# Five groups of projection columns in place of six in a two-layer hybrid decoder, with some tiles reassigned

## The chip, the cores and the metric

The kernel runs on one core of one Trainium2 chip. The metric is device time in microseconds (us) of one execution, lower being better. Inputs and weights, all in single precision, lie in HBM at the start, and the result is written back to HBM.

## The reference

Two layers are applied to a sequence of 256 tokens with 1024 features. In each layer one input projection feeds three groups of heads: mLSTM, MoBA block attention and NSA sparse attention.

```python
for l in range(DEPTH):                                # DEPTH = 2
    h = rmsnorm(x, norm_mix[l])                       # x: 256 x 1024
    proj = h @ w_in[l]                                # w_in: 1024 x 3476
    (m_q, m_k, m_v, m_o, m_i, m_f, b_q, b_k, b_v,     # 4 x 512, 4, 4, 3 x 256
     n_q, n_kc, n_vc, n_ks, n_vs, n_kw, n_vw, n_g) = split(proj)   # 256, 6 x 64, 12
    y_m = mlstm(silu(conv(m_q, m_k)), m_v, m_o, m_i, m_f)
    y_b = moba(b_q, b_k, b_v)
    y_n = nsa(n_q, n_kc, n_vc, n_ks, n_vs, n_kw, n_vw, n_g, cmp_pe[l], ...)
    x = x + concat(y_m, y_b, y_n) @ w_out[l]
    h = rmsnorm(x, norm_ffn[l])
    x = x + square(relu(h @ w_ff1[l])) @ w_ff2[l]     # 1024 -> 4096 -> 1024
```

NSA compresses `n_kc` and `n_vc` with a small network whose inputs get learned positions (`cmp_pe`) added.

## The kernel before, in words

**Matmuls.** Operands are single precision, split into a high part (`hi`, rounded to the format that TensorE takes in one pass) and a low part (`lo`, the rest). A product is three matmuls: high by high, high by low, low by high (`passes`). Tokens are two tiles of 128 (`i` is 0 or 1) and the features are eight tiles of 128 (`k`), so a group of columns that is projected with tokens on the partitions takes 2 x 8 x 3 = 48 matmuls per layer, each with as many moving columns as the group has (`project`).

**Groups.** The 3476 columns of `w_in` are taken in groups (`GROUPS`, line 378): o1 holds NSA's queries and the inputs of its compression (384 columns), o2 the rest of NSA (268: selected and window keys and values, gates), o3 the mLSTM gates and MoBA's queries (264), o4 MoBA's keys and values (512), o5 mLSTM's values (512), o6 its output gate (512). mLSTM's queries and keys are q0 to q3, 256 columns each, projected the other way round (`project_t`: 48 matmuls of 256 columns). c0 to c3 are pieces of the compression network; c0 and c1 run as one burst, and so do c2 and c3. `ORDER` (line 30) is the order on TensorE: o1, o6, o2, o3, c0, c1, q0, c2, c3, o4, q1, q2, q3, o5.

**Weights.** The loads are cut into pieces: four per o group (two feature tiles each), two per q group (four each). A piece is loaded by SP into one of five `raw` tiles (RAW_BUFS, line 32), cast to `hi` by ScalarE (the very first piece by VectorE, in two chunks), and VectorE makes `lo`. There are six tiles of each part. A `raw` tile comes free when the `lo` is made, a part when its last matmul is done. So the load of a piece waits for the `lo` of the piece five earlier. The compression weights go to two `whole` tiles and are not split. One queue, SP's, issues all the weight loads in order.

**PSUM and other tiles.** Results of the o and q groups go to two `acc` banks, other results to six `wk` banks. The two banks of an o group are freed by the process that reads them: `cmp_inputs` (line 899) for o1, `nsa_heads` (line 934) for o2, `gates` (line 1003) for o3, `moba_heads` for o4. `cmp_inputs` copies NSA's queries to two `R` tiles, which `nsa_heads` frees after its normalisation; the pool has only these two. `gates` then takes two `R` tiles for MoBA's queries, so that its copies wait for NSA's normalisation. The `Y` tiles (two) hold mLSTM's output before its transposition (`numerators`). The positions are loaded in `first_smalls` (line 793) to a `dg` tile, after four small loads.

**Order of instructions.** `Flow` is a list planner that runs when the program is written: each process yields operations with planned costs, the planner keeps a planned clock for every engine and issues the operation that can begin first, with preference by rank. Each engine then executes its instructions in that fixed order. `due` (lines 392 to 428) gives each piece a due time, and the casts are placed by it (AHEAD, line 32). The planner's cost of a power on GpSimd, which makes the reciprocal root of `rsqrt`, is 0.3 us and 0.165 us for each value in a row.

**NSA's chain.** For each token tile: copies from PSUM (`R`, `VS`, `GT`), squares (`th`), sums (`hss`), the power (`hr`, on GpSimd), scaling (`N`), rotation, transposes on TensorE to `QK`, and then the scores, a burst of matmuls on `QK`.

Of the kernel before, what the change touches and what calls it, by code (L numbers as in the profile page):

```python
# [26 lines left out]
K_ID, K_TRI, K_NM, K_NMT, K_NMC, K_COS, K_SIN, K_VAL, K_CS, K_END = 0, 128, 256, 384, 512, 544, 576, 608, 612, 868  # L27


ORDER = ("o1", "o6", "o2", "o3", "c0", "c1", "q0", "c2", "c3", "o4", "q1", "q2", "q3", "o5")  # L30

RAW_BUFS, PART_BUFS, AHEAD = 5, 6, 1.3

# [111 lines left out]
class Flow:  # L145
# [25 lines left out]
    def free(self, *tiles):  # L171
        for t in tiles:
            name = t.tensor.name
            self.places[self.owner.pop(name)].append(self.used.get(name, ("", 0.0))[1])
# [108 lines left out]
def body(ctx, tc, x, w_in, b_if, conv_qk, m_norm, moba_g, nsa_qg, nsa_kg, cmp_pe, cmp_w1, cmp_w2,  # L283
# [18 lines left out]
    def new(tag, *shape, dt=F32):  # L302
        return New(tag, (128, *shape), dt)
# [6 lines left out]
    def keep(tag, *shape, dt=F32, parts=128):  # L310

        if tag not in kept:
            kept[tag] = cp.tile([parts, *shape], dt, tag=tag, name=tag)
        return kept[tag]
# [60 lines left out]
    def rows(w, k0, kk, c0, n):  # L375
        return [(w[k0 * 128:(k0 + kk) * 128, c0:c0 + n].rearrange("(k p) n -> p k n", p=128), None)], kk, n

    GROUPS = {"o1": (C_NQ, 384), "o2": (C_KS, 268), "o3": (C_G, 264), "o4": (C_BK, 512), "o5": (C_MV, 512),
              "o6": (C_MO, 512)}
    WO_ORDER = [6, 7, 4, 5, 0, 1, 2, 3]  # L380
    NCH = DFF // 256

# [11 lines left out]
    for l in range(DEPTH):  # L394
        for name in ORDER:
            if name[0] == "c":
                s = int(name[1])
                pieces.append(([(cmp_w1[l, a, s * 512:(s + 1) * 512, :].rearrange("(k p) n -> p k n", p=128), a)
                                for a in range(2)], 8, 128))
                due.append(t)  # L400
                t += 0.45
            elif name[0] == "q":
                pieces += [rows(w_in[l], 4 * s, 4, int(name[1]) * 256, 256) for s in range(2)]
                due += [t, t + 12 * 288 / 2400]
                t += 48 * 288 / 2400
            else:
                n = GROUPS[name][1]
                pieces += [rows(w_in[l], 2 * s, 2, *GROUPS[name]) for s in range(4)]
                due += [t + 6 * s * (n + 32) / 2400 for s in range(4)]
                t += 48 * (n + 32) / 2400  # L410
        pieces += [rows(w_out[l], k, 1, 0, D) for k in WO_ORDER]
        due += [t + 6 * k * 544 / 2400 for k in range(4)] + [t + (48 + 3 * k) * 544 / 2400 for k in range(4)]
        t += 96 * 544 / 2400
        for kind, c, a in FF_ORDER:
            if kind == "up":
                pieces.append(rows(w_ff1[l], 4 * a, 4, c * 256, 256))
                due.append(t)
                t += (8 * 544 + 8 * 288) / 2400
            else:
                if a == 0:  # L420
                    pieces += [rows(w_ff2[l], 2 * c + f, 1, 0, D) for f in range(2)]
                    due += [t, t + 3 * 544 / 2400]
                t += 12 * 544 / 2400

    whole = {j for j, p in enumerate(pieces) if len(p[0]) == 2}
    raws, parts = {}, {}
    coming = [0, 0]
    taken = [0]
# [1 line left out]
    def loads(unsplit):  # L430

        for j, (srcs, kk, n) in enumerate(pieces):
            if (j in whole) != unsplit:
                continue
            if j < 4:
                yield f"before {j}"
            elif unsplit:
                yield f"raw {j - 1}"
            raw = yield new("whole" if j in whole else "raw", 1024)
            raws[j] = raw  # L440
            for src, a in srcs:
                dst = raw[:, :kk * n] if a is None else raw[:, a * 512:(a + 1) * 512]
                yield sy.dma_start(dst.rearrange("p (k n) -> p k n", n=n), src)
            done.add(f"raw {j}")

    def chunks(j):
# [74 lines left out]
    class Layer:  # L521
        def __init__(self):
            self.o, self.held, self.W, self.Y = {}, {}, {}, {}
            self.rs = [keep(f"rs{i}", 1) for i in range(2)]
            self.r2 = [keep(f"r2{i}", 1) for i in range(2)]
            for name, shape, dt in (("H", (8, 2, S), F32R), ("Mh", (8, S), F32R),
                                    ("Ml", (8, S), F32R), ("QK", (10, S), F32), ("RB", (S,), F32),
                                    ("VS", (2, 2, 64), F32), ("VB", (2, 256), F32), ("VM", (2, 4, 130), F32),
                                    ("VC", (4, 64), F32), ("KCT", (2, 16), F32), ("em", (2, 4), F32),
                                    ("cg", (2, 64), F32), ("mr", (384,), F32R)):  # L530
                setattr(self, name, keep(name, *shape, dt=dt))
            self.GT = [keep(f"GT{i}", 12) for i in range(2)]

            self.Hh, self.Hl = (self.H[:, :, a, :] for a in range(2))
            self.Fh, self.Fl = self.Hh, self.Hl

    Ls = [Layer() for _ in range(DEPTH)]

# [253 lines left out]

    def first_smalls():
        yield "H017"
        yield from small_loads(0, 0)
        yield gp.tensor_copy(B[:, 0:128], ident)
        yield gp.tensor_copy(B[:, 128:416], C[:, K_NM - 128:K_NM + 160])
        per = yield new("dg", 128)
        yield sy.dma_start(per[:64], cmp_pe.rearrange("l a (i j) d -> (l a i) (j d)", j=2))
        pps = yield wk()  # L800
        yield tr(pps[:, :64], per[:64], ident[:64, :64])
        yield dv.tensor_copy(PEs, pps[:, :64].rearrange("p (l a i) -> p l a i", l=2, a=2))
        free(pps, per)
        done.add("s00")
        yield "o100"
        yield from small_loads(0, 1)
        done.add("s10")
        for l in range(1, DEPTH):
            yield f"F{l - 1}17"
            for part in range(2):  # L810
                yield from small_loads(l, part)
                done.add(f"s{part}{l}")
# [86 lines left out]
    def cmp_inputs(l):  # L899
        L = Ls[l]  # L900
        L.R = []
        KV = []
        for i in range(2):
            yield f"o1{l}{i}"
            yield f"rs{l}{i}"
            o = L.o["o1"][i]
            KV.append((yield new("KV", 2, 2, 64)))
            yield act(KV[i], o[:, 256:384].rearrange("p (a d) -> p a d", a=2)[:, :, None, :].to_broadcast([128, 2, 2, 64]),
                      AF.Copy, scale=L.rs[i])
            L.R.append((yield new("R", 8, 64)))  # L910
            yield act(L.R[i][:, 0:4].rearrange("p a d -> p (a d)"), o[:, 0:256], AF.Copy, scale=L.rs[i])
            free(o)
            done.add(f"R{l}{i}")
        yield f"s0{l}"

        Xt = yield new("MQ", 2048)
        yield gp.memset(Xt[:, :1024], 0.0)
        X = Xt[:, :1024].rearrange("p (i a c) -> p i a c", i=16, a=2)
        for a in range(2):
            kt = yield wk(S)  # L920
            for i in range(2):
                yield tr(kt[:, tokens(i)], KV[i][:, a].rearrange("p b d -> p (b d)"), ident)
            for j in range(2):
                src = kt[64 * j:64 * j + 64, :]
                src = bass.AP(tensor=src.tensor, offset=src.offset + j, ap=[src.ap[0], [2, 16], [16, NCMP]])
                yield tt(X[64 * j:64 * j + 64, :, a, :NCMP], src,
                         PEs[64 * j:64 * j + 64, l, a, :][:, :, None].to_broadcast([64, 16, NCMP]), op=ALU.add)
            free(kt)
        free(*KV)
        L.Xt, L.X = Xt, X  # L930
        done.add(f"X{l}")


    def nsa_heads(l, i):
# [2 lines left out]
        yield f"o2{l}{i}"  # L937
        yield f"s0{l}"
        o, R, GT = L.o["o2"][i], L.R[i], L.GT[i]
        kv = o[:, 0:256].rearrange("p (a b d) -> p a b d", a=2, b=2)  # L940
        yield act(R[:, 4:6], kv[:, :, 0, :], AF.Copy, scale=L.rs[i])
        yield act(L.VS[:, i], kv[:, :, 1, :], AF.Copy, scale=L.rs[i])

        yield ts(GT, o[:, 256:268], L.rs[i], 0.5, op0=ALU.mult, op1=ALU.mult)
        free(o)
        N = yield new("N", 10, 64)
        yield from normed(N, R[:, 0:6], 6, i, ((0, 4, 2, 1), (4, 2, 4, 2)))
        free(R)
# [54 lines left out]
    def gates(l):  # L1003
# [3 lines left out]
        yield f"s1{l}"  # L1007
        L.R2 = []
        for i in range(2):
            yield f"o3{l}{i}"  # L1010
            yield f"rs{l}{i}"
            o = L.o["o3"][i]
            yield stt(GI[:, i], o[:, 0:8], L.rs[i], BIFs[:, l], op0=ALU.mult, op1=ALU.add)
            L.R2.append((yield new("R", 8, 64)))
            yield act(L.R2[i][:, 0:4].rearrange("p a d -> p (a d)"), o[:, 8:264], AF.Copy, scale=L.rs[i])
            free(o)
            done.add(f"bq{l}{i}")
        fg = GI[:, :, 4:8]
        lf, fa, cg, em, BC = keep("lf", 2, 4), keep("fa", 2, 4), L.cg, L.em, keep("BC", 2, 4)
# [422 lines left out]
```

## Time and profile before

| what | value |
|---|---|
| median of 3 executions | 639.02 us (638.28 to 639.03) |
| the profiled execution | 639.09 us |
| its span, first to last instruction | 637.3 us |
| mean granted TensorE clock | 0.999 of full speed |
| TensorE busy | 629.8 us, 99% of the span, 3799 matmuls |
| VectorE, ScalarE, GpSimd busy | 443.3, 366.6, 30.0 us |
| moved by DMA | 112.78 MB, mean 177 GB/s |

The span lies within the profiled execution's time, with 1.8 us around it. A matmul's record is longer than the distance to the next one, because matmuls are pipelined: the distance between starts, and not the record's length, is what a matmul costs TensorE.

### The profile page before, as it was taken

The numbers are of one execution on the slowest core, as the hardware profiler recorded it, in microseconds if no ns is written. First come the engines' busy times: TensorE is split into PE (matmuls) and PEld (weight loads), VectorE is DVE, ScalarE is ACT, GpSimd is POOL, SyncE is SP. The second block draws the span as 40 slices with busy tenths as digits, with TensorE's granted clock in tenths as the row PEclk, the third lists the DMA queues.
The fourth block names the chain that finished last, engine by engine and source line by source line (L and its number), as shares of the span: only waits on it lengthen the run. The fifth ranks groups of instructions, "written<-read, shape, count | busy, mean of one in ns | idle before, by whom it ended". The sixth has DMA issues, their size and how long they took to land.

```text
span 637.3 us, 10219 instructions
## 1 busy us (share of the span) xinstructions
PE 629.8 (99%) x3799; PEld 544.1 (85%) x3799; DVE 443.3 (70%) x823; ACT 366.6 (58%) x718; POOL 30.0 (5%) x50
## 2 busy tenths in 40 slices
PE   9999999999999999999999999999999999999997
PEld 8898898888888888888899879988888888888885
DVE  6778899678574656656594879987776565665661
ACT  7679685655464535444465886845645554545440
POOL 1010200100000000000010111001000000000000
PEclk9999999999999999999999999999999999999999
DMA  8896524349565565646456924254466556564601
GB/s 310 238 304 210 156 67 140 124 137 284 170 203 194 182 211 160 216 163 200 125 153 212 301 69 142 69 167 152 154 212 212 184 187 209 167 214 156 222 34 67
DMA packets 79378, 112.78 MB, mean 177 GB/s; under 512 B 4928, under 2 KB 61792, under 8 KB 79328
## 3 DMA queue, kind: packets, MB, share of 16 engines
q1 hardware_dynamic: 79152, 112.05, 55.5%
q8 instruction: 30, 0.49, 0.3%
q14 instruction: 20, 0.16, 0.1%
q10 hardware_dynamic: 176, 0.07, 0.0%
HBM read 111.06 MB, written 1.05 MB: 176 GB/s over the span
## 4 chain that ended last, share of the span: by engine, by line
PE 91%; DMA 3%; ACT 2%; DVE 2%; issue 1%; POOL 1%; SPq 0%; ACTq 0%; DVEq 0%; POOLq 0%
PE wk L137 57%; PE acc L137 35%; DMA raw<-in_w_in 2%; ACT hi L137 1%; DVE lo L137 1%; DMA ident<-in_cst 1%; POOL hr L137 0%; SPq L136 0%; DVE N L137 0%; ACT QK L137 0%; POOL rs L137 0%; DVE dg L137 0%; ACT R L137 0%; DVE x L137 0%; DVE hss L137 0%
## 5 line engine op out<-in xcount | busy, mean ns | idle before, releaser
L137 DVE TENSOR_TENSOR lo<-raw,hi 128x1024 fp32r<-128x1024 f32 (+4 forms) x209 | 240.4, 1167 | 123.3 <-ACT hi L137 122.6
L137 ACT CAST hi<-raw 128x1024 fp32r<-128x1024 f32 (+3 forms) x207 | 205.9, 1015 | 135.0 <-PE wk L137 111.7
L137 PE MATMUL wk<-H,hi 128*128 128x512 f32 x512 | 128.0, 391 | 0.0
L137 PEld LDWEIGHTS wk<-H,hi 128*128 128x128 f32 x512 | 93.7, 188 | 17.9
L137 PE MATMUL acc<-hi,H 128*128 128x512 f32 (+3 forms) x368 | 99.2, 351 | 0.0
L137 PE MATMUL acc<-hi,P 128*128 128x512 f32 x240 | 79.3, 391 | 0.2 <-DVE P L137 0.2
L137 PE MATMUL wk<-hi,P 128*128 128x512 f32 x240 | 78.8, 389 | 0.0
L137 PEld LDWEIGHTS wk<-H,lo 128*128 128x128 f32 x512 | 69.9, 190 | 5.0
L137 PE MATMUL wk<-H,lo 128*128 128x256 f32 x512 | 71.4, 282 | 0.0
L137 PEld LDWEIGHTS acc<-hi,H 128*128 128x128 f32 x368 | 64.0, 188 | 6.5 <-issue 0.4
L137 PE MATMUL acc<-lo,H 128*128 128x512 f32 (+3 forms) x184 | 65.3, 355 | 0.0
L137 PEld LDWEIGHTS acc<-hi,P 128*128 128x128 f32 x240 | 45.1, 188 | 9.4 <-DVE P L137 0.6
L137 PEld LDWEIGHTS wk<-hi,P 128*128 128x128 f32 x240 | 45.0, 188 | 9.4
L137 PE MATMUL acc<-H,hi 128*128 128x256 f32 x256 | 51.5, 292 | 0.0
L137 PE MATMUL acc<-lo,P 128*128 128x512 f32 x120 | 47.0, 392 | 0.0
L137 PE MATMUL wk<-lo,P 128*128 128x512 f32 x120 | 46.7, 389 | 0.0
L137 ACT COPY th<-wk 128x256 f32<-128x256 f32 x64 | 23.9, 373 | 35.7 <-PE wk L137 35.7
L137 PEld LDWEIGHTS acc<-H,hi 128*128 128x128 f32 x256 | 40.7, 190 | 0.5 <-ACT hi L137 0.2
L137 PEld LDWEIGHTS acc<-lo,H 128*128 128x128 f32 x184 | 34.6, 188 | 3.4 <-issue 0.3
L137 PE MATMUL acc<-H,lo 128*128 128x256 f32 x128 | 36.7, 287 | 0.0
L137 ACT ACTIVATE H<-wk,V 128x128 fp32r<-128x128 f32 x64 | 18.1, 375 | 21.1 <-PE wk L137 21.1
L137 ACT CAST P<-cv 128x512 fp32r<-128x512 f32 x30 | 18.6, 621 | 17.3 <-DVE cv L137 17.3
(199 smaller groups left out, 799.5 us busy)
## 6 DMA issues: line engine op xcount, KB each, us to landing
raw<-in_w_ff SPq DMA_DIRECT2D x128, 512.0 KB, 4.4
raw<-in_w_in SPq DMA_DIRECT2D x40, 512.0 KB, 5.0
raw<-in_w_out SPq DMA_DIRECT2D x16, 512.0 KB, 4.0
whole<-in_cmp_w SPq DMA_DIRECT2D x16, 256.0 KB, 5.0
raw<-in_w_in SPq DMA_DIRECT2D x8, 384.0 KB, 3.9
raw<-in_w_in SPq DMA_DIRECT2D x8, 268.0 KB, 3.5
raw<-in_w_in SPq DMA_DIRECT2D x8, 264.0 KB, 3.2
out<-x SPq DMA_DIRECT2D x4, 256.0 KB, 2.0
```

The costliest lines, as they stand in the source:

```text
L137: o = Op(self.name, lambda: f(out, *args, **kw), outs, ins, self.cost(op, outs, ins))
```

## The change

The 64 columns of NSA's selected keys go from o2 to o1, and o3 is merged into o2. The groups are now o1 of 448 columns, o2 of 468 (window keys and both values, NSA's gates, then mLSTM's gates and MoBA's queries), and o4, o5 and o6 as before. A piece of o2 comes in two loads, one for each of two runs of columns (204 and 264). A bank of o2 is freed when both `nsa_heads` and `gates` have read it. MoBA's queries go to `Y` tiles, and the positions to a `Y` tile too, with the load issued ahead of the four small ones.

```diff
-ORDER = ("o1", "o6", "o2", "o3", "c0", "c1", "q0", "c2", "c3", "o4", "q1", "q2", "q3", "o5")
+ORDER = ("o1", "o6", "o2", "c0", "c1", "q0", "c2", "c3", "o4", "q1", "q2", "q3", "o5")
...
-    GROUPS = {"o1": (C_NQ, 384), "o2": (C_KS, 268), "o3": (C_G, 264), "o4": (C_BK, 512), "o5": (C_MV, 512),
-              "o6": (C_MO, 512)}
+
+    GROUPS = {"o1": (C_NQ, 448), "o2": (C_KS + 64, 468), "o4": (C_BK, 512), "o5": (C_MV, 512), "o6": (C_MO, 512)}
...
-                pieces += [rows(w_in[l], 2 * s, 2, *GROUPS[name]) for s in range(4)]
+                if name == "o2":
+                    pieces += [([(w_in[l, 256 * s:256 * s + 256, c0:c0 + m].rearrange("(k p) n -> p k n", p=128),
+                                      slice(at, at + m)) for c0, m, at in ((C_KS + 64, 204, 0), (C_G, 264, 204))], 2, n)
+                                   for s in range(4)]
+                else:
+                    pieces += [rows(w_in[l], 2 * s, 2, *GROUPS[name]) for s in range(4)]
...
+            self.left = [2, 2]
...
+        def read(self, i):
+
+            self.left[i] -= 1
+            if not self.left[i]:
+                free(self.o["o2"][i])
...
     def first_smalls():
         yield "H017"
+        per = yield new("Y", 512)
+        yield sy.dma_start(per[:64, :128], cmp_pe.rearrange("l a (i j) d -> (l a i) (j d)", j=2))
         yield from small_loads(0, 0)
         yield gp.tensor_copy(B[:, 0:128], ident)
         yield gp.tensor_copy(B[:, 128:416], C[:, K_NM - 128:K_NM + 160])
-        per = yield new("dg", 128)
-        yield sy.dma_start(per[:64], cmp_pe.rearrange("l a (i j) d -> (l a i) (j d)", j=2))
...
             yield act(L.R[i][:, 0:4].rearrange("p a d -> p (a d)"), o[:, 0:256], AF.Copy, scale=L.rs[i])
+            yield act(L.R[i][:, 4], o[:, 384:448], AF.Copy, scale=L.rs[i])
...
-        kv = o[:, 0:256].rearrange("p (a b d) -> p a b d", a=2, b=2)
-        yield act(R[:, 4:6], kv[:, :, 0, :], AF.Copy, scale=L.rs[i])
-        yield act(L.VS[:, i], kv[:, :, 1, :], AF.Copy, scale=L.rs[i])
-
-        yield ts(GT, o[:, 256:268], L.rs[i], 0.5, op0=ALU.mult, op1=ALU.mult)
-        free(o)
+        yield act(R[:, 5], o[:, 64:128], AF.Copy, scale=L.rs[i])
+        yield act(L.VS[:, i], o[:, 0:256].rearrange("p (a b) -> p a b", a=2)[:, :, 0:64], AF.Copy, scale=L.rs[i])
+
+        yield ts(GT, o[:, 192:204], L.rs[i], 0.5, op0=ALU.mult, op1=ALU.mult)
+        L.read(i)
...
-            yield f"o3{l}{i}"
+            yield f"o2{l}{i}"
             yield f"rs{l}{i}"
-            o = L.o["o3"][i]
-            yield stt(GI[:, i], o[:, 0:8], L.rs[i], BIFs[:, l], op0=ALU.mult, op1=ALU.add)
-            L.R2.append((yield new("R", 8, 64)))
-            yield act(L.R2[i][:, 0:4].rearrange("p a d -> p (a d)"), o[:, 8:264], AF.Copy, scale=L.rs[i])
-            free(o)
+            o = L.o["o2"][i]
+            yield stt(GI[:, i], o[:, 204:212], L.rs[i], BIFs[:, l], op0=ALU.mult, op1=ALU.add)
+            L.R2.append((yield new("Y", 8, 64)))
+            yield act(L.R2[i][:, 0:4].rearrange("p a d -> p (a d)"), o[:, 212:468], AF.Copy, scale=L.rs[i])
+            L.read(i)
```

The rest of the diff lets the loading loop write a run of columns of a piece, and recognises a compression piece by its eight tiles.

## Rows read from the trace of the kernel before

**Rows 1.** The page, parts 1 and 4: busy time and the chain of waits by engine.

```profile
PE 629.8 (99%) x3799; PEld 544.1 (85%) x3799; DVE 443.3 (70%) x823; ACT 366.6 (58%) x718; POOL 30.0 (5%) x50
...
PE 91%; DMA 3%; ACT 2%; DVE 2%; issue 1%; POOL 1%; SPq 0%; ACTq 0%; DVEq 0%; POOLq 0%
```

**Rows 2.** Windows: us, busy time of each engine, clock, DMA share, GB/s.

```profile
28.90:40.60 11.70, 11.70 (x98) 11.64 (x96) 6.06 (x19) 7.05 (x14) 2.15 (x2) 1.00 1.01 327
...
330.50:341.70 11.20, 11.20 (x52) 9.15 (x52) 4.75 (x10) 3.99 (x7) 0.00 (x0) 1.00 0.42 119
341.70:353.50 11.80, 11.80 (x98) 11.62 (x97) 7.71 (x21) 8.07 (x16) 1.62 (x2) 1.00 1.02 349
```

**Rows 3.** Timeline of TensorE, second layer: start us, length us, operation, count.

```profile
323.41 0.33 PE L137 MATMUL acc<-lo,H 128*128 128x384 f32 x1
...
327.05 0.33 PE L137 MATMUL acc<-lo,H 128*128 128x384 f32 x1
...
335.84 0.39 PE L137 MATMUL acc<-lo,H 128*128 128x512 f32 x1
...
341.28 0.39 PE L137 MATMUL acc<-lo,H 128*128 128x512 f32 x1
...
341.86 0.28 PE L137 MATMUL acc<-lo,H 128*128 128x268 f32 x1
...
347.31 0.29 PE L137 MATMUL acc<-lo,H 128*128 128x268 f32 x1
...
347.67 0.28 PE L137 MATMUL acc<-lo,H 128*128 128x264 f32 x1
...
353.17 0.28 PE L137 MATMUL acc<-lo,H 128*128 128x264 f32 x1
```

**Rows 4.** The start: timeline of VectorE, PE and SP, and tiles raw and lo.

```profile
5.35 0.62 DVE L137 CAST hi<-raw 128x384 fp32r<-128x384 f32 x2
...
7.21 0.30 PEld L137 LDWEIGHTS acc<-hi,H 128*128 128x128 f32 x2 [0.18 <-DVE H L137]
...
9.70 0.23 PE L137 MATMUL wk<-B 128*128 128x128 bf16 x1
...
18.56 0.50 SPq L136 DMA_DIRECT2D dg<-in_cmp_pe  x1
...
L137 DVE TENSOR_TENSOR lo<-raw,hi x4: 551/750/959, 5.9 to 11.0; 128x384 fp32r<-128x384 f32 x2, 128x768 fp32r<-128x768 f32 x2
...
DMA to landing us min/median/max: 3.9/3.9/3.9
```

**Rows 5.** The chain of waits in order of time: start us, us, what.

```profile
30.79 8.27 DMA raw<-in_w_in
...
342.12 5.68 DMA raw<-in_w_in
...
353.22 2.63 POOL hr L137
```

**Rows 6.** Timeline of TensorE around three stalls, idle time and releaser in brackets.

```profile
44.21 0.38 PE L137 MATMUL acc<-H,lo 128*128 128x256 f32 x1
44.80 1.16 PE L137 MATMUL wk<-QK 64*128 64x128 f32 x16 [0.21 <-ACT QK L137]
...
356.35 0.28 PE L137 MATMUL acc<-H,lo 128*128 128x256 f32 x1
357.29 0.44 PE L137 MATMUL wk<-ident,N 128*128 128x128 f32 x2 [0.66 <-DVE N L137]
...
358.63 0.28 PE L137 MATMUL acc<-H,hi 128*128 128x256 f32 x1
359.25 1.16 PE L137 MATMUL wk<-QK 64*128 64x128 f32 x16 [0.34 <-ACT QK L137]
```

**Rows 7.** ScalarE's copy of MoBA's queries, second layer, and GpSimd's powers of tile hr.

```profile
353.10 0.47 ACT L137 ACTIVATE R<-acc,rs 128x256 f32<-128x256 f32 x1 [0.37 <-DVE GI L137]
...
L137 POOL TENSOR_TENSOR hr<-hss,negh x8: 1333/1635/2617, 35.8 to 387.0; 128x6 f32<-128x6 f32 x4, 128x8 f32<-128x8 f32 x4
```

More of the change, by code (lines that the diff above doesn't have):

```diff
@@ L423, in body @@
                 t += 12 * 544 / 2400
-    whole = {j for j, p in enumerate(pieces) if len(p[0]) == 2}
+    whole = {j for j, p in enumerate(pieces) if p[1] == 8}
     raws, parts = {}, {}
@@ L441, in loads @@
             for src, a in srcs:
-                dst = raw[:, :kk * n] if a is None else raw[:, a * 512:(a + 1) * 512]
-                yield sy.dma_start(dst.rearrange("p (k n) -> p k n", n=n), src)
+                dst = raw[:, a * 512:(a + 1) * 512] if j in whole else raw[:, :kk * n]
+                dst = dst.rearrange("p (k n) -> p k n", n=n)
+                yield sy.dma_start(dst[:, :, a] if isinstance(a, slice) else dst, src)
             done.add(f"raw {j}")
@@ L797, in first_smalls @@
         yield gp.tensor_copy(B[:, 128:416], C[:, K_NM - 128:K_NM + 160])
-        per = yield new("dg", 128)
-        yield sy.dma_start(per[:64], cmp_pe.rearrange("l a (i j) d -> (l a i) (j d)", j=2))
         pps = yield wk()
-        yield tr(pps[:, :64], per[:64], ident[:64, :64])
+        yield tr(pps[:, :64], per[:64, :128], ident[:64, :64])
         yield dv.tensor_copy(PEs, pps[:, :64].rearrange("p (l a i) -> p l a i", l=2, a=2))
```

## The prediction

> **What bounds the kernel now.** I read the page first. TensorE is busy 99% of the span, and the chain of waits that ends last runs on it for 91% [rows 1]. So a change is worth what it takes from TensorE's own stream of matmuls, plus what it takes from or adds to the few places where that stream stands still. The windows come second, for the stages around the change: the granted clock is 1.00, which is the 2.4 GHz level, and TensorE is busy for the whole of the stretches of o2 and o3 [rows 2]. There the DMA engines are busy too: a share of 1.01 and 1.02, with 327 and 349 GB/s, while the stretch of o6 just before has 0.42 and 119 GB/s in the second layer [rows 2]. Third is TensorE's timeline in the second layer, which gives the distance from one matmul to the next by number of columns [rows 3]. Last are the chain of waits and the timeline around the places where TensorE stood still after o3 [rows 5, 6].
>
> **What a matmul costs.** Rows that show the same operation some periods apart give the distance. 384 columns: 327.05 - 323.41 = 3.64 us for 21 matmuls, 173.3 ns. 512 columns: 341.28 - 335.84 = 5.44 us for 24, 226.7 ns. 268: 347.31 - 341.86 = 5.45 us for 45, 121.1 ns. 264: 353.17 - 347.67 = 5.50 us for 45, 122.2 ns [rows 3]. From 384 to 512 columns the slope is 53.4 / 128 = 0.417 ns a column, one column per cycle at 2.4 GHz, and 13.3 ns of each matmul do not depend on its columns. At 268 and 264 columns the same subtraction leaves 121.1 - 111.7 = 9.4 and 122.2 - 110.0 = 12.2 ns.
>
> **Fewer matmuls.** Three groups of 48 matmuls become two, with the same 916 columns in all. Before, a layer spends 48 x (173.3 + 121.1 + 122.2) = 20.00 us on them. After, with the fixed part of the nearest wide rows, 448 columns cost 186.7 + 13.3 = 200.0 ns and 468 cost 195.0 + 13.3 = 208.3, so 48 x 408.3 = 19.60 us: 0.40 us less. With 9.4 ns as the fixed part, which the rows allow as the low end, it is 48 x 400.5 = 19.22 us: 0.78 us less. 448 is a multiple of 64 as 384 and 512 are, and I give it their part; 468 is not, as 268 isn't, and I give it 9.4: 19.41 us. I take 0.5 us a layer, **1.0 us in two layers**, with ends of 0.8 and 1.6. All of it lies on the path, since TensorE never rests there [rows 2].
>
> A rule of the Trainium skill would make more of this. TensorE: Matmul & The Clock Gate, section Back-to-back issue gap, gives sustained spacings of about 81 ns at 128 columns and 131 ns at 512, which is 64 ns of fixed part, and by it the 96 matmuls saved would be worth an estimated 6.2 us. The same section's formula for an isolated matmul has a fixed 2.5 ns, by which they would be worth an estimated 0.2 us. The rows above, with 226.7 ns at 512 columns, agree with neither, and the sum goes by the rows.
>
> **The first piece.** At the start VectorE casts the first piece in two chunks of 384 columns, 0.62 us for both, and then takes the low parts in two more at 0.551 us each [rows 4]. Low parts of 384 and 768 columns take 551 and 959 ns [rows 4], so 1.06 ns a column, and 64 more columns cost 0.07 us in each of four instructions: 0.27 us. TensorE waits for VectorE just behind them, 0.18 us at 7.21 [rows 4], so this is on the path. Its load has 448 KB in place of 384; it landed 3.9 us after its issue [rows 4], and 64 KB more are 0.2 us at the 327 GB/s of a full stretch [rows 2], so the high end is 0.5. The low end is nothing: at 9.70 a filler matmul runs because the next operands are not there [rows 4], and a later start with more work per piece may only fill that hole. I take **0.2 us more**.
>
> **The loads of q0.** The chain of waits goes through a weight load for 8.27 us in the first layer and 5.68 in the second [rows 5]; both end just ahead of q0's first casts. The reason is in the order of pieces: five raw tiles mean that q0's first load waits for the low part of the piece five earlier, which is o2's last. In the new order the piece five earlier is o6's last, a whole group sooner, and o2's pieces of 468 KB put more bytes into the stretch of o6, where the DMA engines had room [rows 2]. So q0's casts should no longer wait for data, and what stands behind them on ScalarE and VectorE comes earlier.
>
> **The copies of MoBA's queries.** In the second layer ScalarE's copy runs only at 353.10 [rows 7], though o3's first half is done before 351, because the R tile has to come free. In Y tiles it waits for nothing but PSUM and its engine. The bank freed by it is q0's, and the new order leaves the second half of o2 and a burst between, some 6 us, so q0 has no new wait.
>
> **The stalls.** TensorE stands still three times just after the merged groups. From the last regular matmul plus its 120 ns to the next: 44.33 to 44.80 is 0.47 us, 356.47 to 357.29 is 0.82, 358.75 to 359.25 is 0.50, together 1.79 [rows 6]. Two wait for ScalarE's copy of transposed queries, one for NSA's scaled heads. If the loads alone set them, all 1.79 us go; if others of the same kind take their place nothing goes; if NSA's later start doubles them, 1.79 us are added. Behind the longest stands GpSimd's power, 2.63 us in the chain [rows 5] against 1.333 for the shortest [rows 7]; that remains. The first-layer stall is the one nearest to the loads, with only a copy behind casts. I take **0.7 us less**: it goes, and the others shrink by a sixth.
>
> **At no cost.** Four casts and four low parts fewer per layer, each a little wider; two more small copies per layer, each under the 0.47 us of a 256-column one [rows 7]; ScalarE and VectorE are each busy about 8 of 11.8 us there [rows 2]. Without that slack a copy would delay a cast by its length. Loads stay at eight per layer for these groups. On SP the positions' load moves ahead of four small loads and of the weight loads between; its issue takes 0.50 us [rows 4], so those are issued half a microsecond later, covered by o1's and o6's matmuls. The dg tile it no longer holds only helps the row scales.
>
> **Sum.** -1.0 + 0.2 - 0.7 = -1.5 us. The profiled execution took 639.09 us, a span of 637.3 and 1.8 around it, and is 0.07 above the median of 639.02. 639.09 - 1.5 = 637.6.
>
> **The rivals.** *The stalls stay.* The planner fixes the order beforehand, and with other times other matmuls stand early in the queue. Then 639.09 - 1.0 + 0.2 = 638.3, with 637.5 to 638.8 by the bounds of the two terms. For it: the power on GpSimd is still there. Against: the loads of q0 are released a group earlier.
>
> *Slower, by NSA's chain.* The second half of o2 now ends later: in the second layer o1 takes 48 x 26.7 ns = 1.3 us more and o2 10.0 us in place of 5.8, so it ends near 353 and not 347.5, with o3 no longer behind it as cover. Copies, squares, sums, power and scaling of that tile then run beside q0, where scores and transposes of the first tile also go. If the planner again counts the power as about 1.3 us and it takes 2.6 [rows 7], each matmul queued behind is early by 1.3 us. To be slower by more than 0.2% (1.28 us, about what a measurement of this kernel can tell from no change) it takes 1.28 + 0.8 = 2.1 us of new standing still, three stalls of the size of the largest. That would be about 640.5. Against: q0, o4 and q1 are there as filling work, and the first layer had only one such stall.
>
> *All three stalls go*: 639.09 - 1.0 + 0.2 - 1.8 = 636.5. For it: both chains pass through the loads [rows 5].
>
> *The change doesn't do what it says*: wide matmuls cost no more than the 173.3 ns of 384 columns [rows 3]. A layer would save 48 x (416.6 - 346.6) = 3.4 us, giving 639.09 - 6.7 = 632.4. Against: 512 columns take 226.7. The Trainium skill's sustained spacings, in the section named, would point this way.
>
> **How the numbers follow.** The forecast, stalls shrunk, has 0.45 (637.0 to 638.2, mostly below 637.74, the bound of 0.2%); stalls stay 0.34, nearly all within 0.2%; all stalls go 0.11; slower 0.09; cheap wide matmuls 0.01. Faster: 0.36 + 0.02 + 0.11 + 0.01 = 0.50. Within: 0.09 + 0.32 = 0.41. Slower: 0.09. The range runs from 636.3, all stalls gone with the higher saving, to 639.5, stalls kept at the upper bounds and one more of 0.7 us added; it leaves out the slower case and the cheap matmuls. The likeliest case's own range is 637.0 to 638.2.
>
> **What would show it.** In the changed profile: 96 matmuls fewer in these groups, 448 and 468 columns at about 200 and 204 to 208 ns; the first projection matmul about 0.2 us later; q0's casts without a wait for a load; no stall before the first layer's scores; MoBA's queries copied soon after their bank is done. Wrong would be a spacing of 468 columns above 210 ns, new stalls of over 0.8 us before transposes or scores in either layer, or out projections that wait for NSA.

## The result, and the profile after

The kernel after takes 646.67 us (median of 4 runs, 645.87 to 646.98) where the kernel before takes 638.65 in the same comparison: a ratio of 1.0118, with a 95% interval from 1.0104 to 1.0132. It is 8 us slower, and the prediction had 637.6 with a range up to 639.5. The profiled execution took 645.87 us, a span of 644.1.

The page of the kernel after, parts 1, 2 (TensorE's granted clock) and 4, answers to [rows 1]:

```profile
PE 633.2 (98%) x3700; PEld 542.7 (84%) x3700; DVE 444.5 (69%) x815; ACT 368.0 (57%) x714; POOL 31.2 (5%) x50
...
PEclk9988999999999999999999999999999999999999
...
PE 87%; DVE 3%; DMA 3%; ACT 3%; issue 2%; POOL 1%; SPq 0%; ACTq 0%; DVEq 0%; POOLq 0%
```

There are fewer matmuls (3700 in place of 3799, some records missing in both), yet TensorE is busy for 3.4 us longer, and its share of the chain falls from 91% to 87%. The two 8s in the clock say where to look: the slices from 32 to 64 us. The second layer takes no part in the loss. From its first projection matmul to the end of the span it takes 644.09 - 328.47 = 315.62 us, against 637.31 - 320.25 = 317.06 before. All is lost in the first layer, and the windows of the kernel after show it (us, busy time of each engine, clock, DMA share, GB/s; they answer to [rows 2], and the last two are o6 and o2 of the second layer):

```profile
31.00:33.30 2.30, 2.30 (x12) 2.05 (x11) 0.00 (x0) 0.00 (x0) 0.00 (x0) 1.00 0.74 183
33.30:36.90 3.60, 1.42 (x6) 0.67 (x5) 1.25 (x2) 2.46 (x3) 0.00 (x0) 1.00 0.96 268
36.90:40.50 3.60, 3.60 (x11) 3.09 (x10) 1.09 (x2) 0.69 (x1) 0.00 (x0) 0.53 1.05 330
40.60:45.00 4.40, 4.40 (x22) 3.89 (x21) 2.59 (x3) 2.42 (x4) 0.00 (x0) 1.00 1.07 377
50.00:58.00 8.00, 5.98 (x46) 5.54 (x48) 6.54 (x23) 6.87 (x16) 1.81 (x4) 0.79 1.03 315
339.98:351.37 11.39, 11.39 (x54) 9.32 (x52) 6.30 (x11) 4.57 (x7) 0.00 (x0) 1.00 0.71 204
351.37:361.69 10.32, 10.32 (x49) 8.83 (x48) 5.92 (x9) 7.09 (x10) 1.33 (x1) 1.00 0.91 316
```

The merged group of 468 columns takes 10.32 us in the second layer and 14.58 in the first, from 30.98 to 45.56. First TensorE stands still, then it runs at half clock. Its timeline in the first layer (start us, length us, and in brackets the idle time and what ended it):

```profile
33.32 0.38 PE L137 MATMUL acc<-hi,H 128*128 128x468 f32 x1
35.19 0.48 PE L137 MATMUL acc<-hi,H 128*128 128x468 f32 x1 [1.49 <-ACT hi L137]
36.35 0.48 PE L137 MATMUL acc<-lo,H 128*128 128x468 f32 x1 [0.69 <-DVE lo L137]
...
37.25 0.59 PE L137 MATMUL acc<-lo,H 128*128 128x468 f32 x1
...
38.42 0.59 PE L137 MATMUL acc<-lo,H 128*128 128x468 f32 x1
...
52.65 0.44 PE L137 MATMUL wk<-ident,KV 128*128 128x128 f32 x2 [1.85 <-ACT KV L137]
```

The two stops are 1.49 + 0.69 = 2.18 us. After them three matmuls take 38.42 - 37.25 = 1.17 us, 390 ns each, where 213 is the second layer's value; eleven of those are another 1.9 us. A further stop of 1.85 us follows at 52.65, and again a stretch of low clock, 0.79 from 50 to 58.

What ended the first stop is the cast of a weight piece on ScalarE, and what ended the second is the low part of the same piece, made behind that cast. The cast was late because another cast stands ahead of it in ScalarE's order, that of another input (`in_sel`), which waited 4.54 us for its own load. The cast of the next piece then waited 0.65 us for the piece's load:

```profile
33.64 0.62 ACT L137 CAST SEL<-th 128x512 fp32r<-128x512 f32 x1 [4.54 <-DMA th<-in_sel]
34.17 0.97 ACT L137 CAST hi<-raw 128x936 fp32r<-128x936 f32 x1
35.78 0.97 ACT L137 CAST hi<-raw 128x936 fp32r<-128x936 f32 x1 [0.65 <-DMA raw<-in_w_in]
```

The chain of waits in order of time, and SP's timeline, show why these loads were late:

```profile
21.64 3.04 DMA raw<-in_w_in
24.70 0.37 SPq L136
...
25.16 2.83 DMA raw<-in_w_in
28.01 0.37 SPq L136
...
28.47 3.01 DMA raw<-in_w_in
31.50 0.38 SPq L136
...
34.17 6.91 DMA raw<-in_w_in
```

```profile
16.96 11.93 SPq L136 DMA_DIRECT2D raw<-in_w_in  x7
...
29.92 0.43 SPq L136 DMA_DIRECT2D th<-in_sel  x1
...
34.17 2.45 SPq L136 DMA_DIRECT2D raw<-in_w_in  x2
```

The pattern is load, issue, load, issue: SP lets the first load of a pair land before it issues the second. Seven issues take 11.93 us. Each piece of o2 now comes in two loads, 204 and 264 columns wide, into one tile, and the list of waits in the built program has the second of each pair wait for the first:

```
24 L136 DMA raw<-in_w_in 128x2x204 [waits DMAHW1_49,DVE_49]
25 L136 DMA raw<-in_w_in 128x2x264 [waits DMAHW2_49,DMAHW1_49]
```

The `DMAHW` semaphores tell of landings, and it is load 24 whose landing load 25 waits for on `DMAHW1_49`. The two loads write different columns, but with rows of 468 columns the built program has the second wait for the first. In the built program, row lengths of 448, 456, 464, 472 and 480 have no such wait; 460, 466 to 470 and 476 have it. (The program uses eight of these semaphores in turn, so a load also waits for the one eight places ahead of it. That is the other landing in both lists, and the kernel before has such waits too.) Everything behind the pairs on SP is late too. That includes `in_sel`, issued at 29.92, and q0's two loads, issued at 34.17. The chain of waits goes on from q0's load to the stop of 1.85 us:

```profile
41.16 1.06 ACT hi L137
...
49.37 0.47 DVE N L137
...
52.19 0.41 ACT KV L137
```

By the Trainium skill, DMA: Bandwidth & Descriptors, section Anatomy of one DMA — SWDGE (gpsimd) path, the DMA engines themselves do not wait on semaphores; a wait is spent on the issuing sequencer. That section describes loads issued by GpSimd, but the chain's rows on SP agree: the time between two issues is SP's, 2.83 to 3.04 us for each pair.

### The profile page after: what moved, and what is told of

It is laid out like the page before. It is cut to its first block, busy times and chain, and to the rows that moved or that the text cites. A ratio compares the mean times of both kernels' runs of the same rounds, so it can differ in the third digit from the quotient of the medians.

```text
span 644.1 us, 10002 instructions
## 1 busy us (share of the span) xinstructions
PE 633.2 (98%) x3700; PEld 542.7 (84%) x3700; DVE 444.5 (69%) x815; ACT 368.0 (57%) x714; POOL 31.2 (5%) x50
## 4 chain that ended last, share of the span: by engine, by line
PE 87%; DVE 3%; DMA 3%; ACT 3%; issue 2%; POOL 1%; SPq 0%; ACTq 0%; DVEq 0%; POOLq 0%
PE wk L137 54%; PE acc L137 33%; DMA raw<-in_w_in 2%; DVE lo L137 1%; POOL hr L137 1%; DVE N L137 1%; ACT hi L137 1%; ACT P L137 1%; DMA ident<-in_cst 1%; SPq L136 0%; DVE H L137 0%; POOL rs L137 0%; ACT H L137 0%; DVE t L137 0%; ACT Y L137 0%
## 5 line engine op out<-in xcount | busy, mean ns | idle before, releaser
L137 DVE TENSOR_TENSOR lo<-raw,hi 128x1024 fp32r<-128x1024 f32 (+3 forms) x201 | 239.2, 1208 | 132.6 <-ACT hi L137 131.6
L137 ACT CAST hi<-raw 128x1024 fp32r<-128x1024 f32 (+2 forms) x199 | 204.0, 1048 | 131.4 <-PE wk L137 111.7
L137 PE MATMUL acc<-hi,H 128*128 128x512 f32 (+2 forms) x304 | 97.2, 393 | 1.5 <-ACT hi L137 1.5
L137 PEld LDWEIGHTS acc<-hi,H 128*128 128x128 f32 x304 | 57.5, 191 | 11.2 <-ACT hi L137 1.9
L137 PE MATMUL acc<-lo,H 128*128 128x512 f32 (+2 forms) x152 | 60.2, 396 | 0.7 <-DVE lo L137 0.7
L137 PEld LDWEIGHTS acc<-lo,H 128*128 128x128 f32 x152 | 29.0, 191 | 5.6 <-DVE lo L137 1.3
L137 DVE TENSOR_TENSOR cx<-wk,th 128x256 f32<-128x256 f32 x64 | 27.0, 421 | 2.2 <-ACT th L137 2.2
```

Source lines behind the costliest of these rows:

```text
L137: o = Op(self.name, lambda: f(out, *args, **kw), outs, ins, self.cost(op, outs, ins))
```

## Experiments

Each ratio is against the kernel before, run on the same chip in the same batch, with its 95% interval.

**Rows of 472 columns, the wait gone.** The second load takes four more columns, which nobody uses. All else, SP's order included, is that of the kernel after.

```diff
-    GROUPS = {... "o2": (C_KS + 64, 468), ...}
+    GROUPS = {... "o2": (C_KS + 64, 472), ...}
-    ... for c0, m, at in ((C_KS + 64, 204, 0), (C_G, 264, 204))
+    ... for c0, m, at in ((C_KS + 64, 204, 0), (C_G, 268, 204))
```

> The changed kernel with o2's rows 472 columns long in place of 468 (its second run of columns is 268 and not 264; the four added columns are not read afterwards). With 468 the program as built makes the second load of a piece wait until the first has landed; with 472 it does not, and the order of all instructions is the same. Theory A (that wait makes o2's weights late in the first layer, and all the rest follows): the time falls by 7 to 9 us from the changed kernel's 646.7, to 637.5 to 639.5; SP no longer waits for a load, and TensorE's stalls in the first layer's o2 (1.5 and 0.7 us) and the half clock behind them go. Theory B (the wider pieces and twice the loads per piece keep SP and the DMA engines busy too long): 645 or more. Theory C (the planner's order, with the second half of NSA later): only the stretch of o2 recovers, about 5 us, and the stall of 1.9 us before a transpose of KV stays: 641 to 642.5.

Measured: 638.49 us, ratio 0.9988 [0.9977, 1.0]. SP's timeline, the window of o2 in the first layer, and SP's waits for weight loads from 14 to 60 us (us in total, times, longest), here and in the kernel after:

```profile
17.19 4.73 SPq L136 DMA_DIRECT2D raw<-in_w_in  x7
...
27.53 2.05 SPq L136 DMA_DIRECT2D raw<-in_w_in  x2
```

```profile
31.25:41.62 10.37, 10.37 (x49) 8.84 (x47) 6.17 (x10) 7.13 (x10) 1.33 (x1) 1.00 1.06 360
```

```profile
SPq L136 <- DMA raw<-in_w_in: 2.9, 9, 0.7
...
SPq L136 <- DMA raw<-in_w_in: 10.8, 6, 3.8
```

Seven issues take 4.73 us in place of 11.93, `in_sel`'s load is issued at 23.83 in place of 29.92 and q0's at 27.53 in place of 34.17, o2 takes 10.37 us at full clock, and 8 us are gone from the time. SP still waits for weight loads, which the expectation did not have: for those eight places ahead, and never for more than 0.7 us. Wider pieces, two loads a piece and the order of NSA's work are all still there, so none of them made the loss.

**The wait put into the kernel before.** In six groups, o2's pieces come in two loads, once with rows of 270 columns (135 and 135), where the built program waits, once with 272 (136 and 136), where it doesn't.

```diff
-    "o2": (C_KS, 268)
+    "o2": (C_KS - 2, 270)
+    ... slice(at, at + 135)) for at in (0, 135)
```

> The kernel before, with o2's group two columns wider (270, the two in front are not read) and each of its four pieces per layer loaded in two runs of 135 columns, the second of which waits until the first has landed. The other work is that of the kernel before. Theory A: slower than before by 3 to 9 us, with stalls of TensorE in the first layer's o2 or o3, and little in the second layer. Theories B and C: within 1 us of before, as the pieces stay small and the order of NSA stays.

> The same as the run before it with 272 columns, in two runs of 136, which do not wait for each other; the order of SP's loads is the same. Theory A: within 1 us of the kernel before (638.7). If two loads per piece cost by themselves (theory B), it is as slow as the one with 270.

Measured: with 270 columns 645.98 us, ratio 1.0109 [1.0088, 1.0129]; with 272 columns 638.3 us, 0.999 [0.9978, 1.0002]. Two columns decide over 7 us. With 270 the wait shows at another place; the longest waits of TensorE up to 100 us:

```profile
PE wk L137 <- DMA dg<-in_cmp_pe: 5.3, 1, 5.3
```

In the order before, the positions' load stands on SP behind the waiting loads, and TensorE needs it for a transpose. In the kernel after it has been moved ahead of them. So the wait alone costs about as much in six groups, 7.1 us, by a stop that was not the expected one in o2 or o3.

**The tile moves alone.** Six groups, with MoBA's queries in Y tiles and the positions' load in one of these, ahead.

```diff
+        per = yield new("Y", 512)
+        yield sy.dma_start(per[:64, :128], cmp_pe...)
         yield from small_loads(0, 0)
...
-        per = yield new("dg", 128)
...
-            L.R2.append((yield new("R", 8, 64)))
+            L.R2.append((yield new("Y", 8, 64)))
```

> The kernel before with six groups, and of the change only the tiles: MoBA's queries copied to Y tiles and the positions loaded to a Y tile, ahead of the four small loads. Theory A: within 1 us of before, either way, since this part makes no load wait; ScalarE's copy of the queries comes some 3 us earlier in the second layer. If the moved load of the positions delays the weights (a rival to A), slower by 2 us or more with stalls in the first layer.

Measured: 639.46 us, ratio 1.0017 [0.9997, 1.0038]. Nothing gained. The copy of MoBA's queries in the second layer begins 32.63 us after that layer's first matmul, before it was 32.85: the expected 3 us are not there. The profile has one new stop in the first layer:

```profile
PE acc L137 <- DVE GT L137: 1.5, 1, 1.5
```

**Four loads a piece.** Another way to be rid of the wait: one load for each block of 128 rows and each run of columns, so that each writes one unbroken stretch. First at 468 columns, then at 472.

```diff
-    w_in[l, 256 * s:256 * s + 256, c0:c0 + m] ... slice(at, at + m)
+    w_in[l, 256 * s + 128 * k:256 * s + 128 * k + 128, c0:c0 + m] ...
+        slice(k * n + at, k * n + at + m)) for k in range(2)
```

> The kernel after, unchanged in widths (448 and 468 columns), but each piece of o2 comes in four loads, one for each block of 128 rows and each run of columns, so that each writes one unbroken stretch of its tile and none waits for another. Theory A (only the wait of the second load for the first costs the 8 us): the standstill of TensorE at 33 to 37 us goes and the time is 638 to 640 us, as with rows of 472, a little above for eight more issues of some 0.4 us on SP in each layer. Rival B (468 columns, or two sources for one tile, cost by themselves): it stays near 646 us.

> Five groups with rows of 472 columns, each piece of o2 in four loads, one for each block of 128 rows and each run of columns; no load waits for another of its piece. It differs from the 644.77 us of the four loads at 468 in the row's length alone, and from the 638.49 us of the two loads at 472 in the number of loads and in the order that the planner writes for them. Theory D (twice as many loads, behind which the others of the queue come later, cost the 5 to 6 us): 643 to 646 us. Rival B (468 columns cost by themselves): 638 to 639.5 us.

Measured: 644.77 us, ratio 1.0098 [1.0078, 1.0118], at 468; 644.52 us, 1.0072 [1.005, 1.0094], at 472. The first expectation failed for both theories: the loss is there without the wait. The second run clears the row length, since 472 loses as much. The loss has moved, too. In the run at 472, o2 of the first layer takes 10.38 us (30.79 to 41.17), and TensorE stops behind it:

```profile
32.00 14.89 SPq L136 DMA_DIRECT2D raw<-in_w_in  x9
```

```profile
43.30 0.47 PE L137 MATMUL acc<-H,hi 128*128 128x256 f32 x2 [1.06 <-DVE GT L137]
50.47 0.44 PE L137 MATMUL wk<-ident,N 128*128 128x128 f32 x2 [1.31 <-DVE N L137]
51.74 0.44 PE L137 MATMUL wk<-ident,KV 128*128 128x128 f32 x2 [0.83 <-ACT KV L137]
53.38 0.69 PE L137 MATMUL wk<-ident,N 128*128 128x128 f32 x2 [1.08 <-DVE N L137]
```

```profile
50.00:54.00 4.00, 1.61 (x8) 0.85 (x8) 3.94 (x18) 3.19 (x6) 1.78 (x4) 0.83 1.08 331
54.00:58.00 4.00, 4.00 (x41) 3.40 (x41) 3.30 (x13) 3.26 (x9) 0.00 (x0) 0.50 0.96 316
```

On SP stand sixteen loads where eight stood, so q0's first load is issued at 32.0 us, not at 27.5. ScalarE waits for it, and the timeline of ScalarE has q0's casts ahead of the copies that start NSA's chain:

```profile
39.29 1.05 ACT L137 CAST hi<-raw 128x1024 fp32r<-128x1024 f32 x1 [4.66 <-DMA raw<-in_w_in]
40.71 1.05 ACT L137 CAST hi<-raw 128x1024 fp32r<-128x1024 f32 x1 [0.36 <-DMA raw<-in_w_in]
```

Heads scaled late (N), gates late (GT), copies late (KV): 4.28 us of stops, and 4 us at half clock behind them. In this execution GpSimd's power of 128 x 6 elements at 46.66 us also took 2.37 us, where the next one took 1.34, so up to 1.0 us of the first stop for N may be its doing. Eight more issues of 0.43 us on SP make 3.4 of the 4.5 us by which q0's load is late. The planner also wrote another order for these two kernels, with two loads ahead of q0's (1.03 and 1.26 us) that stand behind it in the run with two loads, and that part is not separated from the number of loads.

**Six groups in the first layer, five in the second.** All five-group code, rows of 472 included, is switched on for the second layer alone.

```diff
-        for name in ORDER:
+        for name in ORDERS[l]:
```

> First layer in six groups with all as in the kernel before, second layer in five groups with rows of 472 columns, MoBA's queries of the second layer in the output tiles. Theory A with the stage starts read so far (five groups cost some 0.9 us in the first layer, mostly at the start, and gain some 1.4 us in the second, mostly stalls of NSA's stage): 637.2 to 638.0 us, 0.9 to 1.5 us below the kernel before. Rival (the stalls that went in the second layer hang on the first layer's timing, and come back): 638.6 to 639.2 us.

Measured: 639.44 us, ratio 1.0 [0.9989, 1.0011], near the rival's time, but not for the rival's reason. The stalls of the second layer do not come back: no wait of TensorE there is over 0.3 us, and the layer takes 316.06 us against 317.06 before. It is the first layer that is longer in this execution. It has the same instructions in the same order as the kernel before on TensorE, VectorE, ScalarE and SP, yet the second layer begins at 321.61 us, not at 320.25. So the same first layer can differ by 1.4 us from one execution to another, and a gain of that size read from one pair of profiles proves nothing. The first layer's waits differ from those of [rows 6]:

```profile
42.93 0.44 PE L139 MATMUL wk<-ident,KV 128*128 128x128 f32 x2 [0.62 <-ACT KV L139]
...
44.21 0.44 PE L139 MATMUL wk<-ident,N 128*128 128x128 f32 x2 [0.30 <-DVE N L139]
```

**Spacing by width.** Five groups, rows of 472; in the second layer, the matmuls of o6, o4 and o5 at inner indices 1 to 6 take fewer columns, so parts of the products of these groups are left out.

```diff
+            m = WIDTHS.get((l, name), {}).get(k, n)
-            yield from passes(po[i][:, :n], hx, lx, wh[:, k % 2, :], ...)
+            yield from passes(po[i][:, :m], hx, lx, wh[:, k % 2, :m], ...)
```

> The kernel with five groups and rows of 472, but in the second layer the matmuls of o6, o4 and o5 at inner indices 1 to 6 take fewer columns (o6: 496, 480, 464, 456, 448, 440; o4: 432, 416, 400, 384, 352, 320; o5: 288, 280, 272, 268, 264, 256), which leaves products of the projection out. It measures the start-to-start spacing by width within one execution. The prediction's step (fixed part of about 13 ns from 384 columns up, 9 to 12 at 268 and 264): 448 at 200 ns, 464 at 206 ns, 480 at 213 ns. The rival reading of the runs so far (a fixed part of 15 to 18 ns between 448 and 472): 202.5, 211.5 and 215 ns or more. The time is some 6 us lower by the columns left out, 632 to 633 us.

Measured: 632.28 us in one execution, and these distances from one matmul to the next of the same width (medians of 3 to 48): 268 columns 125 ns, 320: 147, 384: 173, 448: 203, 464: 212, 472: 215, 480: 217, 496: 223. Without the columns at 2.4 GHz that leaves about 13, 14, 13, 16, 19, 18, 17 and 16 ns. All but 448 and 472 have only three or four distances, so a few ns are uncertain there. Still the part that does not depend on the columns isn't constant: 9 to 14 ns up to 384 columns, with [rows 3], and 16 to 19 from 448 to 496. It does not simply grow with the columns, for 512 have 13.3 in [rows 3]; why, no run shows. Rows further apart in the run with 472 columns say the same of 448 and 472 (second layer, start and length, 12 and 45 matmuls apart):

```profile
325.88 0.36 PE L137 MATMUL acc<-lo,H 128*128 128x448 f32 x1
...
328.32 0.36 PE L137 MATMUL acc<-lo,H 128*128 128x448 f32 x1
...
344.21 0.38 PE L137 MATMUL acc<-lo,H 128*128 128x472 f32 x1
...
353.85 0.38 PE L137 MATMUL acc<-lo,H 128*128 128x472 f32 x1
```

2.44 us / 12 = 203 ns and 9.64 / 45 = 214 ns; the rival's readings.

**The first piece in two loads.** One for each block of 128 rows, in five groups with rows of 472 (run twice) and in six.

```diff
+                if j == 0:
+                    for k in range(kk):
+                        yield sy.dma_start(dst[:, k], src[:, k])
+                    continue
```

> The kernel with five groups and rows of 472, but the very first piece comes in two loads, one for each block of 128 rows. Theory S1 (the first group starts later because its first cast waits for a larger load): the first cast begins 0.3 to 0.8 us earlier and the time falls by 0.3 to 0.8 us, to about 637.9 us. Rival S2 (at the start the DMA engines are full, and the 64 KB more in each piece of the first group are what is late): the first cast begins earlier, but o6's first matmul stays at 18.9 to 19.3 us and the time within 0.3 us of 638.5 us or above.

> The kernel before, in six groups, with its very first piece in two loads, one for each block of 128 rows. Theory: the first cast begins some 1 us earlier and the time falls by 0.3 to 0.8 us, as it did by 0.5 us in five groups: 638.0 to 638.6 us where the kernel before takes 638.9. Rival (what ends last at the start is x or the DMA engines as a whole): no change that can be told.

> Five groups, rows of 472 columns, first piece in two loads, once more, beside the six groups with their first piece in two loads: what five groups are worth by themselves, the start being cut in the same way in both. Theory (fewer matmuls are worth 0.1 us, not 1.0, and the stalls move with each execution): within 0.5 us of the six groups. Rival (the prediction's 1 us of fewer matmuls is there): 0.9 us or more below the six groups.

Measured: five groups 638.17 us, ratio 0.998 [0.9968, 0.9993], and again 638.19, 0.998 [0.9965, 0.9994]; six groups 639.22, 0.9992 [0.9976, 1.0008]. In five groups VectorE's first cast begins 1.49 us earlier than in the run with 472 columns and one load, and some 1.0 us earlier than in the other kernels with one load, where it begins at 5.46 to 5.60 us. The row of one load at 472 columns, then that of two:

```profile
5.99 0.70 DVE L137 CAST hi<-raw 128x448 fp32r<-128x448 f32 x2 [0.50 <-DMA raw<-in_w_in]
```

```profile
4.50 0.39 DVE L137 CAST hi<-raw 128x448 fp32r<-128x448 f32 x1 [3.50 <-DMA raw<-in_w_in]
```

But the first projection matmul begins no earlier, at 7.20 and 7.58 us against 6.28 to 6.79 with one load, and o6 begins at 18.58 and 18.97 us, against 18.68 to 19.16. From 0.9988 with one load to 0.998 with two is the half microsecond of the first theory, but the intervals overlap and the profiles do not show where it would come from. In six groups no change can be told, as the rival had it. The version with five groups, rows of 472 and the first piece in two loads is the fastest of the study, some 1.2 us below the kernel before and over 8 below the kernel after. What five groups are worth by themselves is not settled. Side by side they are 1.03 us below the six (638.19 and 639.22), the rival's figure; against the kernel before it is 0.998 and 0.9992, whose intervals overlap; and with the first piece in one load the five groups of 472 columns, at 638.49 us, were not below the six groups with 272, at 638.30. The second layer has no part in any gain: from its first projection matmul to the end of the span it takes 315.59 to 315.65 us in five executions with five groups and 315.58 to 315.85 in four with six. (Three others were longer, 316.06 and 316.48 with five and 317.06 with six.)

## Why the prediction was wrong

**The step that failed** is in the part at no cost: "Loads stay at eight per layer for these groups." The count holds: o2 and o3 had four loads each, and the merged o2 has eight. But they fill four tiles now, two loads a tile, and the second of each pair waits for the first to land. The step counted issues and took them for free of each other. It had SP's queue in view for the positions' load, but not a wait inside the queue, nor what stands behind it there. In the first layer that wait is 2.8 to 3.0 us a pair on SP. By way of `in_sel`, whose cast holds up ScalarE, it brings 2.18 us of stops and 1.9 us of half clock in o2, and by way of a late q0 a stop of 1.85 us and more low clock after. From the start of o2 to the out projection the kernel after takes 124.40 - 30.98 = 93.42 us and the kernel with rows of 472 117.06 - 31.25 = 85.81: 7.6 of the 8 us.

In the second layer the same waits stand in the program, and they cost nothing: SP is far enough ahead there, TensorE's longest wait after 60 us is 0.3 us, and o2 takes 10.32 us.

**Fewer matmuls: -1.0 predicted, -0.1 measured.** 448 columns take 203 ns and 468 take 213 ((361.17 - 351.58) / 45 in the kernel after), so a layer spends 48 x 416 = 19.97 us on them where it spent 20.00. The step took the fixed part from the nearest rows, 13.3 and 9.4 ns, and at these widths it is 16 to 18. The Trainium skill's sustained spacings in TensorE: Matmul & The Clock Gate, section Back-to-back issue gap, would have made an estimated 6.2 us of it; no run shows that. The estimated 0.2 us by the same section's formula are near the measured 0.1, though not for its reason: it has 2.5 ns of fixed part where the rows have 9 to 18.

**The first piece: +0.2 predicted, about +0.6.** In the kernels with five groups and a first piece in one load, o6 begins at 18.68 to 19.16 us (five executions), in six groups at 16.77 to 16.94 (five): 2.0 us later in the mean. In the second layer, where nothing is late, the wider o1 takes 11.46 us in place of 10.07, so 1.4 of the 2.0 are columns and 0.6 are the start, just above the high end of 0.5. What the 0.6 are made of isn't shown: with the first piece in two loads o6 begins at 18.58 and 18.97 us, hardly earlier.

**The stalls: -0.7 predicted, nothing shown.** The two second-layer stalls of [rows 6] come after a power on GpSimd that took 2.63 us in that execution [rows 5]. In the run with 272 columns, which has that stage unchanged but for o2's width, the same power shows as

```profile
353.38 1.38 POOL L137 TENSOR_TENSOR hr<-hss,negh 128x6 f32<-128x6 f32 x1 [3.69 <-DVE hss L137]
```

and the stalls aren't there: its second layer takes 635.89 - 320.25 = 315.64 us with six groups, and the kernel after, with five, 315.62. In the six groups with the first piece in two loads it is the same: 1.38 us for the power, no such stall, 315.85 us. So the 1.4 us between the two profiles' second layers are not the worth of five groups; most likely the execution of the kernel before happened to be long there. There is only one profile of that kernel itself, so this is not shown, nor is it that the long power made it so: it was not changed by itself.

**The reasons behind that term** held in part. In the run with 472 columns q0's casts wait for no load in the second layer, where one of them waited 0.68 us before; in the first layer they still wait 0.63 and 0.69 us, before 1.41 and 0.58. And the copy of MoBA's queries was not late for want of an R tile: in the run with the tile moves alone, where it goes to a Y tile, it came 0.2 us earlier.

**The rival of NSA's chain** had the right kind of stop for a part of the loss: a wait of 1.85 us for KV in the kernel after, and waits of 0.83 to 1.31 us for N, KV and GT in the run with four loads at 472, where it had three of 0.7 us. The stops in o2 and the low clock it did not have. But the trigger that it named, the later end of o2's second half, was not the cause. With rows of 472 that later end is there and no such loss; with q0's loads issued 4.5 us later, or 6.6, there is.

**The signs named beforehand.** Two of the three that would show the prediction wrong came true: a spacing of 468 columns above 210 ns (213), and stops of over 0.8 us before transposes (1.85).

**Without the wait** the time comes near the forecast, and that is luck. 0.9988 of the kernel before is 0.8 us less, with an interval from 1.5 less to nothing, where 1.5 less were forecast. But the terms as measured are -0.1 and about +0.6, with nothing shown for the stalls, and add up to 0.5 us more. Where the difference comes from, no run shows.

## What to carry to other kernels

Where a diff turns one load into two for the same tile, list the waits of the built program before anything else: a load that waits for the load ahead of it in its own queue costs a whole landing, 3 us here, and holds everything queued behind. Here the first stop came through another input that stood behind the pairs, and a later one through the next group's weights. Pad the row so that the wait goes (468 to 472 columns gave 8 us back), rather than cut the loads smaller (four loads a piece lost 5 to 6 us). And before a stall of under a microsecond is put into a sum, look for it in a second execution: the two in the second layer here were not there in four other kernels with six groups.

## What the runs showed of the hardware

In the kernel after, TensorE was busy for 1.42 us from 33.30 to 36.90, with stops of 1.49 and 0.69 us. In the 3.6 us after, the granted clock was 0.53, nearly all of it at the 1.2 GHz level, and 468 columns took 390 ns in place of 213. In the run with four loads at 472, TensorE was busy for 1.61 of 4 us, and the 4 us after had a clock of 0.50. In both the slow clock came on top of the stop, 1.9 us on top of 2.18 in the first.

The part of a matmul's distance that doesn't depend on its columns was 9 to 14 ns up to 384 columns and 16 to 18 at 448, 468 and 472, so merging groups saved next to nothing. A power of 128 x 6 elements on GpSimd, at the same place of the second layer, took 2.63 us in the kernel before and 1.38 with 272 columns.
